# Small products of a hybrid attention and RWKV-7 layer, written with the whole 128 x 128 array

## The chip, the cores and the metric

The kernel runs on one core of a Trainium2 chip. The metric is device microseconds of one launch, the median of several runs; lower is better. A profile of one execution on the chip is read beside it. In it PE is the tensor engine's matmul, PEld its weight load, DVE the vector engine, ACT the scalar engine, POOL the GpSimd engine and SP the engine that issues most DMAs.

## The reference

One layer for 1024 tokens of width 1024. A combined projection feeds a sparse attention (eight heads) and an RWKV-7 recurrence (eight heads of 64); their outputs go through one output projection, and a feed-forward block of width 4096 follows. Cut to what the change touches:

```python
def dsa_attention(q, c_kv, q_idx, k_idx, w_idx, ...):
    inv_rms_k = lax.rsqrt(jnp.mean(k_full * k_full, axis=-1) + RMS_EPS)
    ...
    rel = jax.nn.relu(jnp.einsum('bthd,bsd->bths', qi, k_idx))      # index scores, 8 heads of 64
    score_idx = jnp.einsum('bth,bths->bts', wi, rel)
    score_idx = jnp.where(key_pos[None, :] < limit[:, None], score_idx, -jnp.inf)
    _, sel = lax.top_k(score_idx, 256)
    ...

def rwkv7_time_mix(p, ...):
    w_log = -jax.nn.softplus(-(w0 + jnp.tanh(xw) @ w2)) - 0.5
    decay = jnp.exp(-jnp.exp(w_log))
    a = jax.nn.sigmoid(a0 + xa @ a2)                                # xa: 64 columns
    kk = heads(k * k_k)
    kk = kk / jnp.maximum(jnp.sqrt(jnp.sum(kk * kk, axis=-1, keepdims=True)), 1e-12)
    def step(state, inp):
        sa = einsum('bhij,bhj->bhi', state, -kk_t)
        state = state * w_t + sa[..., None] * (kk_t * a_t) + v_t[..., None] * k_t
        return state, einsum('bhij,bhj->bhi', state, r_t)
    ...

def reference(x, c, ...):
    h = rms_norm(x, g_mix) * (1 + sc1) + sh1
    proj = h @ w_in
    x = x + gt1 * (concat([o_a, o_b]) @ w_out)
    h = rms_norm(x, g_ffn) * (1 + sc2) + sh2
    u = relu(h @ w_ff1)
    return x + gt2 * ((u * u) @ w_ff2)
```

## The kernel before

Tokens are worked on in two halves of 512. **The large products** (`dense`, `load_w`) keep weights stationary: a block of 128 x 128 weights is split into a high part `whi` (made by ACT) and a low part `wlo` (made by POOL or DVE), and the 512 tokens' activations, split likewise (`hh`, `hl`; in the feed-forward `uh`, `ul`), stream past. Each block gives three products of 128 rows, 128 columns and 512 streamed elements, here called dense products; there are 4608 of them and their PSUM tile is `ps_mm`. A product of plain float32 tiles stands in the trace as two hardware matmuls, one of the split tiles as one.

**The recurrence** (`rwkv_proj`, `rwkv_feat`, `rwkv_feat2`, `rwkv_inv`, `rwkv_chain`, `rwkv_out`) runs per half for four pairs of heads, each pair in eight chunks of 64 tokens. A chunk is a loop of dependences between PE and DVE: the products `Mt x Vbd` and `KR x H` fill `px`; DVE copies it to `Xb` (L659); the product with the inverse `TT` gives `pu` (L660), which DVE copies to `UV` (L661) and ACT to `Ub` (L663); the product of `BKn` and `UV` gives `ph`, with which DVE renews the state `H` (L669), on which the next chunk's `KR x H` waits. The product of `Lb` and `Ub` (L665, into rows 64 to 127 of `px`) gives the output, which ACT copies to `On`. `rwkv_inv` prepares the inverse `TT` of the next pair, mostly on DVE (`Y`, `ytmp`, L616 and L618).

**Sums of squares** per head (`stat`, L434) multiply by a matrix of 8 columns, one product for each pair of heads, 24 in all; `attn_proj` has two more with one column (the latent's sum, `pc`). **The second low-rank input** `xa` is multiplied by the 64 rows of `a2` (L516), once for each pair, 8 in all.

**The indexer** (`indexer`) scores 512 queries of each half against the keys, head by head. For each head and each block of 128 queries and up to 512 keys there are two products into `ps_f`: `qs x kiH`, where `qs` holds the queries' high parts in rows 0 to 63 and their low parts in rows 64 to 127 and `kiH` the keys' high parts twice, and `qs[0:64] x kiL`, of 64 rows. ACT takes the relu to `rl`, DVE adds it to the scores `sc` (L840). There are 80 such pairs of products, 16 in the first half and 64 in the second. After them comes a search for the 256th largest score, bit by bit, on DVE and ACT, then the attention.

What stands beside what on an engine is set by a scheduler of the framework when the kernel is built: every engine works off a fixed list in order. Between the small products of the recurrence and the indexer it puts dense products of the projections and of the first half's feed-forward. The second half's feed-forward stands last, with nothing else beside it.

Of the kernel before, what the change touches and what calls it, by code (L numbers as in the profile page):

```python
# [4 lines left out]
F32 = mybir.dt.float32  # L5
# [46 lines left out]
# column layout of the packed per-partition parameters  # L52
# [8 lines left out]
# column layout of the constants (they depend on shapes alone)  # L61
CC = {}
_n = 0
for _name, _w in (("ident", 128), ("oblk", 128), ("tri", 128), ("ind", 32), ("zmask", 128), ("yinit", 256),
                  ("dmat", 128), ("cdiag", 128)):
    CC[_name] = (_n, _w)
    _n += _w
NCC = _n
NCF = CC["zmask"][0]    # the columns before are needed as float32


def make_consts():
# [3 lines left out]
    def put(name, a):  # L76
        o, w = CC[name]
        c[:, o:o + w] = a
# [17 lines left out]
    ind = np.zeros((128, 4, 8))  # L96
    for j in range(4):
        ind[:64, j, 2 * j] = 1
        ind[64:, j, 2 * j + 1] = 1
    put("ind", ind.reshape(128, 32))  # L100
# [10 lines left out]
def body(tc, I, out, dbg=None):  # L111
# [21 lines left out]
    # ---------------------------------------------------------------- pools  # L133
# [11 lines left out]
    # ---------------------------------------------------------------- constants and parameters  # L145
# [25 lines left out]
    def power(t):  # L171
        """t**-0.5 in place"""
        G.tensor_tensor(t, t, mhalf.to_broadcast(list(t.shape)), ALU.pow)

    def newton(x, y, t):
        """y = x**-0.5 by Newton's steps from the halved bits"""
# [8 lines left out]
    def sigmoid(out, x, bias=0.0):  # L185
        """sigmoid(x + 2*bias) = (1 + tanh(x/2 + bias))/2"""
        A.activation(out, x, AF.Tanh, scale=0.5, bias=bias)
        EN(8).tensor_scalar(out, out, 1.0, 0.5, ALU.add, ALU.mult)
# [19 lines left out]
    a2w = cst.tile([128, 512], F32, name="a2w")  # L208
    nc.sync.dma_start(a2w[64:128], I["a2"])
# [5 lines left out]
    # persistent state  # L215
# [8 lines left out]
    # DRAM scratch  # L224
# [14 lines left out]
    # ---------------------------------------------------------------- modulation  # L239
# [6 lines left out]
    g1 = per.tile([128, 16], F32, name="g1")   # g*(1+sc) for the two norms  # L246

    def modulation4(j, q, pool, tag):
        """mod[:, 8j+4q ... 8j+4q+3], from 512 columns of w_ada"""
# [17 lines left out]
    def modulation_v(j, q, pool, tag):  # L267
        """the same, with the products away from the tensor engine"""
# [22 lines left out]
    # ---------------------------------------------------------------- x^T, norm, h^T  # L291
# [13 lines left out]
    def norm_first(hf, xp, xn, nb, tags):  # L305
        """x^T, each token over its rms, to the eight tiles of xn"""
# [37 lines left out]
    def norm_T(xT, n, n2, xp, hp):  # L344
        """the norm of x^T: sums over d by the tensor engine, four column groups at a time"""
# [16 lines left out]
        # over all partitions: out[d, t] = sum over t' of r1[t'] * (t' == t)  # L362
# [12 lines left out]
    # ---------------------------------------------------------------- dense product, weights stationary  # L375
    def load_w(w, row0, col0, M):
        """four row blocks of weights, as hi and lo"""
# [23 lines left out]
    # ---------------------------------------------------------------- RWKV-7  # L401
# [30 lines left out]
    def stat(ps, src, j):  # L432
        """sums over each head's rows of pair j, as rows 2j and 2j+1"""
        mmul(ps[0:8, :], C("ind", 8 * j, 8 * j + 8), src, start=(j == 0), stop=(j == 3))  # L434

    def inverse(ps, i, sl, scale, eps):
        """the -0.5th power of max(sum, eps) or of scale*sum + eps for eight rows of sums; to rnd[i]"""
# [17 lines left out]
    def rwkv_proj(hf, hT):  # L455
        """projections of group B, shifted; r, k, v to DRAM; the inverse norms of k*k_k"""
# [29 lines left out]
    def rwkv_feat(hf, j, L4, rp, bp):  # L486
        """features of head pair j; what the even pairs need lies in rp, so that they can run ahead"""
# [17 lines left out]
        # per-token decay exponents in natural layout  # L505
# [10 lines left out]
        mmul(pa, a2w[64:128, j * 128:j * 128 + 128], xa[64:128, :])  # L516
        # a = (1 + at)/2
# [30 lines left out]
        # kappa * W_{t-1}, with W_{-1} = 1 at a chunk's first token  # L548
# [50 lines left out]
    def rwkv_inv(hf, j, R, rp):  # L599
        mark('inv%d%d' % (hf, j))  # L600
        Lb, TT = R["Lb"], R["TT"]
# [46 lines left out]
    def rwkv_chain(hf, j, R, rp):  # L648
# [4 lines left out]
        for c in range(8):  # L653
# [6 lines left out]
            mmul(pu[0:64, 0:128], TT[:, c, :], flat(Xb))  # L660
            (A.copy if CE[1] == "a" else V.tensor_copy)(UV[0:64, c, :], pu[0:64, 0:128])  # L661
            for h in range(2):
                (V.tensor_copy if CE[2] == "v" else A.copy)(Ub[h * 64:h * 64 + 64, h, :], pu[0:64, h * 64:h * 64 + 64])  # L663
            mmul(ph[:, 0:128], BKn[:, c, :], UV[:, c, :])
            mmul(px[64:128, 0:128], Lb[:, c, 1, :], flat(Ub), start=False, stop=True, tile_position=(0, 64),  # L665
                 skip_group_check=True)
# [32 lines left out]
    # ---------------------------------------------------------------- sparse attention  # L699
    def attn_proj(hf, hT, rt):  # L700
        """projections of group A: q^, k^, v and the indexer's q and k to DRAM"""
# [26 lines left out]
        # latent, keys and values  # L728
# [6 lines left out]
        mmul(pc[0:1, :], ones128[:, 0:1], sq)  # L735
# [38 lines left out]
        # indexer keys and weights  # L774
# [14 lines left out]
    def indexer(hf, ap, mp):  # L789
        """additive masks (0 or -1e30) of the half's four query blocks"""  # L790
# [23 lines left out]
        kiL = ap.tile([64, SW], F32R, name="kiL", tag="kiL", bufs=1)  # L814
        A.copy(kiH[:, 0:SW], kir[:, 0:SW])
        V.tensor_tensor(kiL[:, 0:SW], kir[0:64, 0:SW], kiH[0:64, 0:SW].bitcast(F32), ALU.subtract)
# [3 lines left out]
        for h in range(8):  # L820
# [5 lines left out]
            for b in blocks:  # L826
                W = width(b)
                s_ = sc[b]
                for c0 in range(0, W, 512):
# [4 lines left out]
                    mmul(ps[:, 0:n], qs[0:64, tq], kiL[:, c0:c0 + n], start=False, stop=True)  # L834
# [9 lines left out]
        # the 256th largest score of each row, bit by bit in the order of the floats. The vector engine counts  # L844
        # (x >= c); the scalar engine sums sign(x - c), which is #(x > c) + #(x >= c) - W and so finds that score
# [439 lines left out]
```

## Time and profile before

| | |
|---|---|
| median of 3 runs | 1831.04 us (1826.63 to 1836.64) |
| span of the profiled execution | 1829.8 us |
| PE busy | 1661.3 us (91%), 8388 matmuls |
| PEld busy | 1200.9 us (66%) |
| DVE busy | 1160.2 us (63%) |
| ACT busy | 867.0 us (47%) |
| POOL busy | 467.8 us (26%) |
| granted TensorE clock, mean | 0.962 |

The profile gives the span from the first to the last instruction of its execution and no longer time for it; the median of the runs is 1.2 us above that span. The ends of matmuls are modelled, so a matmul's listed duration runs into the next one; the time that a product takes of the engine is read from the starts of successive products. An operation named `ps_f<-kiL,iqs 64*128 64x512` is a product into the tile `ps_f` that uses 64 rows and 128 columns of the array (`64*128`) and streams 512 elements.

### The profile page before, as it was taken

What the parts mean: (1) busy time and instruction counts of PE and PEld (TensorE: products, weight loads), DVE (VectorE), ACT (ScalarE), POOL (GpSimd) and SP (SyncE); (2) the same over time, 40 slices, a digit from 0 to 9 for tenths busy, and PEclk for the clock granted to TensorE, in tenths of its full rate; (3) what the DMA queues carried; (4) which work ended last, traced back from release to release, by engine and by line L of the source; (5) the groups of instructions that cost most, each with busy time, mean ns of one, the idle gap of its engine ahead of it and who ended that gap; (6) DMA issues with size and microseconds to landing.
All of it is one profiled execution on the core that took longest, in us unless ns stands there. A gap on an engine that the chain in (4) does not pass through costs nothing. (4 is left out here: it accounts for less than half of the span.)

```text
span 1829.8 us, 25015 instructions
## 1 busy us (share of the span) xinstructions
PE 1661.3 (91%) x8388; PEld 1200.9 (66%) x8388; DVE 1160.2 (63%) x2981; ACT 867.0 (47%) x1760; POOL 467.8 (26%) x390
## 2 busy tenths in 40 slices
PE   5997889898978988989997789799999999999998
PEld 2674546556653656656555668577786788888887
DVE  4777789845898868986579956877212343333333
ACT  4323353443556655335664687576425252525251
POOL 2445322323241142333312344110344300000000
PEclk9997999998989999999998899899999999999999
DMA  9795344224334643111311223341532343333332
GB/s 311 255 286 181 87 140 144 74 70 133 98 94 149 193 142 106 45 47 47 87 35 52 65 80 110 93 110 47 167 98 74 88 138 93 98 93 98 97 94 75
DMA packets 279366, 205.53 MB, mean 112 GB/s; under 512 B 33811, under 2 KB 234643, under 8 KB 279238
## 3 DMA queue, kind: packets, MB, share of 16 engines
q1 hardware_dynamic: 268482, 184.68, 34.1%
q10 hardware_dynamic: 10628, 19.24, 2.9%
q8 instruction: 66, 1.08, 0.2%
q14 instruction: 62, 0.51, 0.1%
q0 software_dynamic: 128, 0.01, 0.0%
HBM read 175.11 MB, written 28.78 MB: 111 GB/s over the span
## 5 line engine op out<-in xcount | busy, mean ns | idle before, releaser
L384 POOL TENSOR_TENSOR wlo<-wraw,whi 128x512 fp32r<-128x512 f32 x256 | 338.5, 1326 | 737.6 <-ACT whi L382 625.9
L120 PE MATMUL ps_mm<-hh,whi 128*128 128x512 f32 (+1 forms) x1024 | 423.2, 414 | 21.7 <-ACT ur L1061 6.9
L382 ACT CAST whi<-wraw 128x512 fp32r<-128x512 f32 x384 | 235.5, 616 | 400.6 <-PE ps_mm L120 383.7
L120 PE MATMUL ps_mm<-hl,whi 128*128 128x512 f32 (+1 forms) x1024 | 421.7, 412 | 3.6 <-DVE hl L328 1.9
L120 PE MATMUL ps_mm<-hh,wlo 128*128 128x512 f32 (+1 forms) x1024 | 421.0, 411 | 0.7 <-POOL wlo L384 0.6
L120 PEld LDWEIGHTS ps_mm<-hh,whi 128*128 128x128 f32 (+1 forms) x1024 | 197.7, 194 | 79.8 <-issue 20.2
L120 PEld LDWEIGHTS ps_mm<-hl,whi 128*128 128x128 f32 (+1 forms) x1024 | 197.7, 193 | 54.9 <-issue 13.9
L120 PEld LDWEIGHTS ps_mm<-hh,wlo 128*128 128x128 f32 (+1 forms) x1024 | 198.1, 193 | 50.9 <-issue 12.3
L120 PE MATMUL ps_mm<-uh,whi 128*128 128x512 f32 x512 | 207.3, 406 | 15.3 <-DVE acc L895 10.0
L120 PE MATMUL ps_mm<-ul,whi 128*128 128x512 f32 x512 | 206.8, 404 | 2.0 <-DVE ul L1077 2.0
L120 PE MATMUL ps_mm<-uh,wlo 128*128 128x512 f32 x512 | 206.1, 403 | 0.7 <-POOL wlo L384 0.6
L384 DVE TENSOR_TENSOR wlo<-wraw,whi 128x512 fp32r<-128x512 f32 x128 | 88.2, 689 | 130.8 <-ACT whi L382 130.8
L874 ACT ACTIVATE jka<-sc,canda 128x1024 bf16<-128x1024 f32 (+1 forms) x93 | 90.2, 970 | 87.9 <-DVE canda L872 68.2
L120 PEld LDWEIGHTS ps_mm<-uh,whi 128*128 128x128 f32 x512 | 98.0, 192 | 40.5 <-ACT jka L874 10.8
L1083 DVE SCALAR_TENSOR_TENSOR xT<-ps_mm,mod,xT 128x512 f32<-128x512 f32 x64 | 47.9, 749 | 108.5 <-PE ps_mm L120 108.4
L120 PEld LDWEIGHTS ps_mm<-ul,whi 128*128 128x128 f32 x512 | 98.1, 192 | 25.5 <-DVE ul L1077 2.8
L120 PEld LDWEIGHTS ps_mm<-uh,wlo 128*128 128x128 f32 x512 | 98.2, 192 | 24.9 <-issue 1.8
L1077 DVE TENSOR_TENSOR ul<-ur,uh 128x512 fp32r<-128x512 f32 x64 | 47.9, 748 | 71.8 <-ACT uh L1076 71.7
L618 DVE TENSOR_TENSOR Y<-Y,ytmp 128x60 f32<-128x60 f32 (+24 forms) x248 | 75.7, 305 | 6.2
L616 DVE TENSOR_TENSOR ytmp<-Lu,Y 128x60 f32<-128x60 f32 (+24 forms) x248 | 72.6, 293 | 6.1
L982 DVE CUSTOM_DVE_ANT_0 L<-ps_f,mk 128x512 f32<-128x512 f32 (+3 forms) x96 | 52.0, 552 | 26.2 <-PE ps_c L1000 15.6
L988 ACT ACTIVATE L<-L,m 128x128 f32<-128x128 f32 (+7 forms) x64 | 49.7, 777 | 30.9 <-DVE m L985 21.0
(319 smaller groups left out, 2563.6 us busy)
## 6 DMA issues: line engine op xcount, KB each, us to landing
wraw<-in_w_ff_dram SPq DMA_DIRECT2D x256, 256.0 KB, 2.8
wraw<-in_w_in_dram SPq DMA_DIRECT2D x92, 256.0 KB, 3.4
mraw<-in_w_ada_dram SPq DMA_DIRECT2D x64, 256.0 KB, 5.0
mraw<-in_w_ada_dram SPq DMA_DIRECT2D x16, 512.0 KB, 10.7
wraw<-in_w_out_dram SPq DMA_DIRECT2D x32, 256.0 KB, 2.9
rkvd<-shy ACTq DMA_DIRECT2D x24, 256.0 KB
xin<-in_x_dram SPq DMA_DIRECT2D x8, 512.0 KB, 5.5
v<-rkvd SPq DMA_DIRECT2D x16, 256.0 KB
```

The lines of the kernel that those rows point to most:

```text
L120: r = T.matmul(out, lhsT, rhs, start=start, stop=stop, **kw)
L382: (A.copy if HE[GRP[0]] == "a" else V.tensor_copy)(hi[:, :, 0:M], raw[:, :, 0:M])
L384: (V if LE[GRP[0]] == "v" or LE[GRP[0]] == "m" and GRP[1] else G).tensor_tensor(lo[:, :, 0:M], raw[:, :, 0:M], hi[:, :, 0:M].bitcast(F32), ...
L616: V.tensor_tensor(tv, Lu[:, c, 0:c].unsqueeze(2).to_broadcast([128, c, n]), Y[:, c, t0:8].unsqueeze(1).to_broadcast([128, c, n]), ALU.mult)
L618: V.tensor_tensor(Y[:, 0:c, t0:8], Y[:, 0:c, t0:8], tv, ALU.subtract)
L874: A.activation(jka[:, 0:width(b)], sc[b], AF.Sign, scale=-1.0, bias=0.0 if bit == 31 else canda.bitcast(F32)[:, i:i + 1], accum_out=ca[:, ...
L982: V.tensor_tensor_reduce(L[:, c0:c0 + n], ps[:, 0:n], masks[b][:, c0:c0 + n], 1.0, -3e38, ALU.add, ALU.max, m2[:, pc:pc + 1])
L988: A.activation(L[:, 0:W], L[:, 0:W], AF.Exp, bias=m2[:, 2:3], accum_out=m2[:, 3:4])
L1077: V.tensor_tensor(b, r, a.bitcast(F32), ALU.subtract)
L1083: V.scalar_tensor_tensor(xT[:, d, :], ps, mod[:, 40 + d:41 + d], xT[:, d, :], ALU.mult, ALU.add)
```

## The change

Six kinds of product that used 64 rows, or 64, 8 or 1 columns of the array, are written with 128 rows and 128 columns. What is added is zero rows, or columns whose results nobody reads:

- `stat`: the 8-column matrix becomes a slice of 128 columns out of 134, zero but for two columns, so that the rows 2j and 2j+1 of the sums stay where they were; all 128 rows of the PSUM tile are written and 8 read.
- `a2`: `a2w` gets 64 zero rows by a memset, and `xa` is loaded with all 128 rows (256 KB for 128 KB, twice).
- the product with `TT`: the weights are the 64 columns of chunk c and the 64 of chunk c+1 (`TT` has a ninth, zero block), and 64 of 128 result rows are read.
- the product with `Lb`: the weights are both 64-column halves of `Lb`; the results of the unread half are added to rows 0 to 63 of `px`, which have been copied by then.
- `pc`: 128 columns of ones for one.
- the indexer's second product: `kiL` is made for 128 rows instead of 64, and multiplies all of `qs`. (Here the added rows are not zero: they add the product of the two low parts.)

The rest of the diff takes out comments and docstrings, which moves a line number by one from L120 on.

```diff
-                  ("tri", 128), ("ind", 32), ("zmask", 128), ...
+                  ("tri", 128), ("ind", 134), ("zmask", 128), ...
...
-    ind = np.zeros((128, 4, 8))
-    for j in range(4):
-        ind[:64, j, 2 * j] = 1
-        ind[64:, j, 2 * j + 1] = 1
-    put("ind", ind.reshape(128, 32))
+    ind = np.zeros((128, 134))
+    ind[:64, 6] = 1
+    ind[64:, 7] = 1
+    put("ind", ind)
...
+    G.memset(a2w[0:64], 0.0)
     nc.sync.dma_start(a2w[64:128], I["a2"])
...
-        mmul(ps[0:8, :], C("ind", 8 * j, 8 * j + 8), src, start=(j == 0), stop=(j == 3))
+        mmul(ps, C("ind", 6 - 2 * j, 134 - 2 * j), src, start=(j == 0), stop=(j == 3))
...
-        mmul(pa, a2w[64:128, j * 128:j * 128 + 128], xa[64:128, :])
+        mmul(pa, a2w[:, j * 128:j * 128 + 128], xa)
...
-            mmul(pu[0:64, 0:128], TT[:, c, :], flat(Xb))
+            mmul(pu[:, 0:128], flat(TT[:, c:c + 2, :]), flat(Xb))
...
-            mmul(px[64:128, 0:128], Lb[:, c, 1, :], flat(Ub), start=False, stop=True, tile_position=(0, 64),
-                 skip_group_check=True)
+            mmul(px[:, 0:128], flat(Lb[:, c, :, :]), flat(Ub), start=False, stop=True, skip_group_check=True)
...
-        mmul(pc[0:1, :], ones128[:, 0:1], sq)
+        mmul(pc, ones128, sq)
...
-        kiL = ap.tile([64, SW], F32R, name="kiL", tag="kiL", bufs=1)
+        kiL = ap.tile([128, SW], F32R, name="kiL", tag="kiL", bufs=1)
         A.copy(kiH[:, 0:SW], kir[:, 0:SW])
-        V.tensor_tensor(kiL[:, 0:SW], kir[0:64, 0:SW], kiH[0:64, 0:SW].bitcast(F32), ALU.subtract)
+        V.tensor_tensor(kiL[:, 0:SW], kir[:, 0:SW], kiH[:, 0:SW].bitcast(F32), ALU.subtract)
...
-                    mmul(ps[:, 0:n], qs[0:64, tq], kiL[:, c0:c0 + n], start=False, stop=True)
+                    mmul(ps[:, 0:n], qs[:, tq], kiL[:, c0:c0 + n], start=False, stop=True)
...
-        nc.sync.dma_start(xa[64:128], xwd[64:128, sl])
+        nc.sync.dma_start(xa, xwd[:, sl])
...
-        TT = [TT0, bp.tile([128, 8, 64], F32, name="TT1")]
+        TT = [TT0, bp.tile([128, 9, 64], F32, name="TT1")]
...
-    TT0 = rp.tile([128, 8, 64], F32, name="TT0")
+    TT0 = rp.tile([128, 9, 64], F32, name="TT0")
```

The scheduler writes other lists for the changed products. On PE, in the fifth chunk of the second pair of heads of the second half, this stands before from the product of `UV` to the next product of `H` (a row gives the result's rows and columns):

```order
L120 MATMUL ps_c<-UV,BKn 128x128
L120 MATMUL ps_o<-Ub_5738,Lb 64x128
L120 MATMUL ps_mm<-hh,whi 128x512
L120 MATMUL ps_mm<-hl,whi 128x512
L120 MATMUL ps_mm<-hh,wlo 128x512
L120 MATMUL ps_o<-Vbd,Mt 128x128
L120 MATMUL ps_mm<-hh,whi 128x512
L120 MATMUL ps_mm<-hl,whi 128x512
L120 MATMUL ps_o<-H_119,KR 128x128
```

And this stands there in the changed kernel:

```order
L119 MATMUL ps_c<-UV,BKn 128x128
L119 MATMUL ps_o<-Ub_5739,Lb 128x128
L119 MATMUL ps_mm<-hh,whi 128x512
L119 MATMUL ps_mm<-hl,whi 128x512
L119 MATMUL ps_o<-Vbd,Mt 128x128
L119 MATMUL ps_mm<-hh,wlo 128x512
L119 MATMUL ps_mm<-hh,whi 128x512
L119 MATMUL ps_o<-H_120,KR 128x128
```

One dense product fewer stands between the two. Over all chunks 65 dense products leave the recurrence for later places: ahead of the second half's first product with `kiL` stand 1508 dense products before and 1443 now, and the two lists are level again at the 2832nd, in the middle of the feed-forward blocks. In the second half's index scores, PE's list before reads, at the 49th to 52nd product with `kiL`:

```order
L120 MATMUL ps_f<-kiH,iqs 128x512
L120 MATMUL ps_f<-kiL,iqs 128x512
L120 MATMUL ps_mm<-uh,whi 128x512
L120 MATMUL ps_f<-kiH,iqs 128x128
L120 MATMUL ps_f<-kiL,iqs 128x128
L120 MATMUL ps_mm<-ul,whi 128x512
L120 MATMUL ps_mm<-uh,wlo 128x512
L120 MATMUL ps_f<-kiH,iqs 128x512
L120 MATMUL ps_f<-kiL,iqs 128x512
L120 MATMUL ps_f<-kiH,iqs 128x256
L120 MATMUL ps_f<-kiL,iqs 128x256
```

And now:

```order
L119 MATMUL ps_f<-kiH,iqs 128x512
L119 MATMUL ps_f<-kiL,iqs 128x512
L119 MATMUL ps_mm<-hl,whi 128x512
L119 MATMUL ps_mm<-hh,wlo 128x512
L119 MATMUL ps_f<-kiH,iqs 128x128
L119 MATMUL ps_f<-kiL,iqs 128x128
L119 MATMUL ps_f<-kiH,iqs 128x512
L119 MATMUL ps_f<-kiL,iqs 128x512
L119 MATMUL ps_f<-kiH,iqs 128x256
L119 MATMUL ps_f<-kiL,iqs 128x256
```

The pairs of products come in the same order, with other dense products beside them; in the whole stretch from the first to the last product with `kiL` of this half there are 71 dense products in both lists.

## Rows read from the trace of the kernel before

**Rows 1.** Page, busy time of each engine, share of the span, instructions.
```profile
PE 1661.3 (91%) x8388; PEld 1200.9 (66%) x8388; DVE 1160.2 (63%) x2981; ACT 867.0 (47%) x1760; POOL 467.8 (26%) x390
```
**Rows 2.** Stretches: busy us of each engine (instructions), granted clock, DMA share, GB/s.
```profile
core 0: us, PE busy (x) PEld busy (x) DVE busy (x) ACT busy (x) POOL busy (x), PEclk, DMA share, GB/s
210.00:360.00 150.00, 132.29 (x824) 83.11 (x823) 132.60 (x422) 68.32 (x182) 44.78 (x38) 0.99 0.39 118
380.00:420.00 40.00, 39.80 (x199) 25.39 (x198) 16.62 (x54) 17.84 (x46) 8.97 (x7) 0.98 0.20 54
665.00:865.00 200.00, 180.85 (x1146) 120.67 (x1144) 166.20 (x467) 92.06 (x227) 60.34 (x49) 0.97 0.22 64
889.50:954.50 65.00, 65.00 (x199) 34.09 (x198) 47.27 (x75) 41.53 (x81) 9.50 (x7) 1.00 0.14 41
954.50:1050.00 95.50, 74.37 (x277) 57.57 (x278) 92.19 (x267) 50.56 (x92) 30.12 (x22) 0.88 0.20 58
447.50:473.50 26.00, 25.98 (x76) 15.31 (x77) 18.85 (x26) 14.92 (x29) 6.45 (x5) 0.87 0.31 92
```
**Rows 3.** Chain that ended last: start us, us, what.
```profile
1475.04 334.24 PE ps_mm L120 x1457
```
**Rows 4.** Timeline, PE, second half's index scores: start us, us, product.
```profile
920.21 0.39 PE L120 MATMUL ps_f<-kiH,iqs 128*128 128x512 f32 x1
920.52 0.50 PE L120 MATMUL ps_f<-kiL,iqs 64*128 64x512 f32 x1
920.95 0.49 PE L120 MATMUL ps_f<-kiH,iqs 128*128 128x512 f32 x1
921.38 0.50 PE L120 MATMUL ps_f<-kiL,iqs 64*128 64x512 f32 x1
921.80 0.50 PE L120 MATMUL ps_mm<-ul,whi 128*128 128x512 f32 x1
922.14 0.39 PE L120 MATMUL ps_mm<-uh,wlo 128*128 128x512 f32 x1
```
**Rows 5.** Timeline, PEld, two microseconds on: start us, us, weight load, idle before.
```profile
922.14 0.19 PEld L120 LDWEIGHTS ps_f<-kiH,iqs 128*128 128x128 f32 x1
922.68 0.18 PEld L120 LDWEIGHTS ps_f<-kiL,iqs 64*128 64x128 f32 x1 [0.35 <-issue]
```
**Rows 6.** Tile kiL: product, count, ns min/median/max, first and last start, forms.
```profile
L120 PE MATMUL ps_f<-kiL,iqs x80: 324/492/792, 447.9 to 954.3; 64*128 64x512 f32 x48, 64*128 64x384 f32 x16, 64*128 64x128 f32 x8, 64*128 64x256 f32 x8
```
**Rows 7.** Timeline, PE, a chunk of the second half's third pair of heads.
```profile
788.62 0.38 PE L120 MATMUL ps_o<-H,KR 128*128 128x128 f32 x2
788.76 0.48 PE L120 MATMUL ps_mm<-hh,whi 128*128 128x512 f32 x1
789.07 0.40 PE L120 MATMUL ps_mm<-hl,whi 128*128 128x512 f32 x1
...
789.53 0.40 PE L120 MATMUL ps_mm<-hh,whi 128*128 128x512 f32 x1
789.77 0.40 PE L120 MATMUL ps_mm<-hl,whi 128*128 128x512 f32 x1
790.10 0.43 PE L120 MATMUL ps_c<-Xb,TT 128*64 128x128 f32 x2
790.46 0.50 PE L120 MATMUL ps_mm<-hh,wlo 128*128 128x512 f32 x1
790.80 0.40 PE L120 MATMUL ps_mm<-hh,whi 128*128 128x512 f32 x1
```
**Rows 8.** Waits of PE: us in total, times, longest us.
```profile
PE ps_c L120 <- DVE Xb L659: 11.3, 14, 3.1
PE ps_c L120 <- DVE UV L661: 4.2, 8, 1.2
```
**Rows 9.** Weight loads by shape: line, operation, shapes, count | busy us, mean ns | idle before.
```profile
L120 PEld LDWEIGHTS ps_o<-Ub,Lb 128*64 128x64 f32 x128 | 12.5, 138 | 13.6 <-ACT Ub L663 6.3 <-issue 2.6 <-ACT whi L382 0.9
L120 PEld LDWEIGHTS ps_c<-Xb,TT 128*64 128x64 f32 x128 | 12.2, 135 | 37.3 <-DVE Xb L659 26.1 <-issue 6.1 <-ACT BKn L597 1.7
L120 PEld LDWEIGHTS ps_dx<-asq,con 128*8 128x8 f32 x32 | 1.5, 87 | 12.7 <-ACT asq L712 10.8 <-ACT kr L764 0.8 <-issue 0.6
```

More of the change, by code (lines that the diff above doesn't have):

```diff
@@ L63 @@
 _n = 0
-for _name, _w in (("ident", 128), ("oblk", 128), ("tri", 128), ("ind", 32), ("zmask", 128), ("yinit", 256),
+for _name, _w in (("ident", 128), ("oblk", 128), ("tri", 128), ("ind", 134), ("zmask", 128), ("yinit", 256),
                   ("dmat", 128), ("cdiag", 128)):
@@ L600, in rwkv_inv @@
         mark('inv%d%d' % (hf, j))
-        Lb, TT = R["Lb"], R["TT"]
+        Lb, TT = R["Lb"], R["TT"][:, 0:8, :]
         Ld = rp.tile([128, 8, 32], F32, name="Ld", tag="Ld", bufs=1)
```

## The prediction

> **What bounds the kernel now.** I read the page's busy times first, then busy time by stretches, the chain that ended last, PE's timeline in two places, and the waits. PE is busy 91% of the span, no other engine over 63% [rows 1]. From 1475 us on the chain holds almost nothing but dense products: 1457 of them in 334.24 us, 0.229 us each [rows 3]. That is the pace of a PE that never waits, and time saved ahead of this tail shortens the span in full. The reader should look for what lies above that pace earlier.
>
> In the second half's index scores (889.5 to 954.5 us) PE is the bound: busy 65.0 of 65.0 us, against 47.3 for DVE and 41.5 for ACT [rows 2]. In the recurrence PE and DVE are close: 132.3 and 132.6 of 150 us, 180.9 and 166.2 of 200; only in the last pair of the first half (380 to 420) has DVE room, with 16.6 of 40 [rows 2]. The search after the scores belongs to DVE, with 92.2 of 95.5 us [rows 2].
>
> **What a small product costs today.** Take the starts in the scores: 920.21, 920.52, 920.95, 921.38, 921.80, 922.14 [rows 4]. Five products take 1.93 us; at 0.229 they would take 1.15. The extra 0.78 us belongs to four changes between 128 rows and 64, so 0.196 us each. The parts can be seen: from `kiH` to `kiL` 0.31 (0.08 over the pace: the array empties first), from `kiL` to the next 0.42 or 0.43 (its own weights are loaded in sight, and the array empties again), and after the change back 0.34 (a full-size product that also had to wait for its weights). On PEld the load for `kiL` begins only at 922.68, after 0.35 us of idleness put down to no releaser [rows 5]; loads between equal shapes begin one product ahead.
>
> In the recurrence `H,KR`, which has the full shape, and the dense product behind it take 0.45 us together (788.62 to 789.07); `Xb,TT` with 64 columns and the one behind it take 0.70 (790.10 to 790.80), and ahead of it 0.33 passes instead of 0.24 [rows 7]. So such a product costs 0.34 us more than a full one, if PE isn't waiting for data anyway.
>
> **The change part by part**, on PE's time first:
> - `kiL`: 64 products in the second half's scores, 16 in the first (80 in all [rows 6]), two changes of shape each. 128 x 0.196 = 25.1 us and 32 x 0.196 = 6.3 us. The 128 rows stream no longer than 64, since only the streamed elements count.
> - `Xb,TT` and `Ub,Lb`: 64 products each (128 hardware matmuls in each row [rows 9]). 128 x 0.34 = 43.5 us at most. Where PE stands waiting, nothing is gained in front, and the wider load costs 0.19 [rows 5] less 0.135 to 0.138 [rows 9], some 0.055 us more. PE waits so for `Xb` 14 times, 11.3 us, and for `UV` 8 times, 4.2 us [rows 8].
> - 24 sums and the 2 of the latent: 0.39 for two changes less 0.10 for a load of 128 columns instead of 8 (0.19 against 0.087 [rows 5, 9]), some 0.3 each, 7.8 us.
> - `a2`: 8 x 0.39 = 3.1 us. Its memset, the doubled load of `xa` (twice 128 KB more) and 102 more columns of constants are ready long before use, and DVE's `kiL` is two instructions on more partitions at the same length; I cost them at nothing, at most 1 us together.
>
> Together 85.8 us of PE time. What of it reaches the end:
> - Second half's scores: PE needs 65.0 - 25.1 = 39.9, less than DVE's 47.3 [rows 2]. DVE ends last now: between 47.3 and 65, and I take 50, since PE has two `ps_f` banks and DVE will not be fed without gaps. -15.
> - First half's scores: 26.0 - 6.3 = 19.7, against DVE's 18.9 [rows 2]: -5.
> - Recurrence: DVE has 17.4 and 33.8 us idle in the two long stretches [rows 2]. Its idle time is where it waits for PE in the loop; half of it, 25.6, is a guess between nothing and all. In the pair at 380 us, where DVE has room, 8 x 2 x 0.34 = 5.4. Together -31.
> - 65 dense products leave the recurrence for the feed-forward, where PE has nothing to hide them: 65 x 0.229 = +14.9. Part of the 31 is thus only moved.
> - Sums, latent and `a2`: half of 10.9, as the sums also wait for ACT's squares (10.8 us of idle loads [rows 9]): -5.5.
>
> Sum: -15 - 5 - 31 + 14.9 - 5.5 = -41.6. The profiled execution's span of 1829.8 becomes 1788.2. The median lies 1.2 above the span, so I forecast **1789 us**.
>
> What is late next: in the scores DVE's accumulation (L840). In the recurrence the wait for `Xb`, behind which PE's list holds `Xb,TT` and two or three dense products, and behind these `UV,BKn`, for which `H` and thus the next chunk waits. The search starts earlier and is no shorter.
>
> The Trainium skill, "TensorEngine Tiling (Array Packing)", section "Key Properties", says that tiles of the array work independently, so that a weight load and a matmul in different tiles run side by side. It speaks against this change: by it a 64-row product would run beside its neighbour, and filling the array would give that up. The starts in the scores don't bear it out, as `kiL` holds its successor back by 0.43 us and not by less than 0.229.
>
> **Rivals.**
> 1. The recurrence gives nothing net: the loop of copies and waits sets its time, and what it loses is only the moved dense products. For it: DVE at 88% in the first stretch and the 22 waits [rows 2, 8]. Against: the 0.33 us ahead of `Xb,TT` with its successor ready [rows 7]. Then -15 - 5 - 5.5: 1806.
> 2. PE's list decides almost everywhere, and all but the scores' DVE limit comes back: 15 + 6.3 + 43.5 + 10.9 = 75.7: 1755. For it: the waits for `Xb` and `UV` are only 15.5 us [rows 8]. Against: DVE would have no idle time left.
> 3. Slower: PE now waits more in the recurrence and its clock is granted less often. The search shows it: PE busy 74 of 95.5 us, granted clock 0.88, against 0.97 to 0.99 in the recurrence [rows 2]. PE's 353 busy us there (132 + 40 + 181) would become 353 x (0.98/0.88 - 1) = 40 us longer; with the moved 14.9 us and 128 x 0.055 = 7 us of wider loads, against 25.5 saved elsewhere, +36: 1867. From a clock of about 0.94 downwards (353 x (0.98/0.94 - 1) = 15, and 15 + 22 - 25.5 = +11) it decides the sign. Against it: the same columns stream in less time, which leaves PE no idler than now.
> 4. The change doesn't do what it says: small products cost nothing by their shape and run beside their neighbours. Then 80 full products are added, 80 x 0.229 = 18, and the loads 7: 1856. Only the 0.34 us after each `kiL` [rows 4], which belongs to a full-shape product, speaks strongly against it, and it is enough. It is what the page cited above would lead to.
>
> **Chances.** Forecast 0.60 (its own range 1774 to 1798), rival 1 0.20, rival 2 0.09, rival 3 0.06, rival 4 0.05. A difference of 0.5%, 9 us, is about what a measurement of this kernel can tell from none. Faster by more holds the forecast, rival 2 and most of rival 1, whose 25 us allow for a reshuffled list that costs 16: 0.87. Within 0.5%: 0.06, from rival 1's slow end and 3 and 4 half-way. Slower: 0.07. The range of 1760 to 1817 leaves out most of rival 2 and the slower cases.
>
> **What would show it.** In the profile after: `kiH`, `kiL` and dense products starting 0.23 us apart where nothing waits, and the loads for `kiL` one product ahead; the scores' stretch at 48 to 53 us with DVE nearly full; behind `Xb,TT` 0.45 us instead of 0.70; more of PE's waits put down to `Xb` and `UV`; a longer stretch of pure dense products at the end, by some 15 us. The forecast is wrong if the starts after `kiL` keep the 0.34, if the scores stay at 65 us, if the recurrence's eight pairs take as long as now, or if the granted clock there falls below 0.94.

## The result, and the profile after

The changed kernel takes 1808.04 us (median of 4 runs, 1806.42 to 1810.30) against 1829.9 us for the kernel before (4 runs, 1826.63 to 1836.64): a ratio of 0.9878, with an interval of 0.9859 to 0.9898. That is 22 us faster; the forecast was 42. The profiled execution's span went from 1829.8 to 1804.6 us, and its granted clock from 0.962 to 0.966.

The page's busy times answer to [rows 1]: PE loses 47.5 us, PEld and DVE stay within 6 us, ACT loses 7.5 us and POOL gains 12.5.

```profile
PE 1613.8 (89%) x8388; PEld 1206.4 (67%) x8388; DVE 1159.7 (64%) x2981; ACT 859.5 (48%) x1760; POOL 480.3 (27%) x391
```

The same stretches as in [rows 2], found by the same products (recurrence of the first half, its last pair, recurrence of the second half, second half's scores, the search's first 98 us, first half's scores), in the same columns:

```profile
210.80:352.60 141.80, 121.64 (x801) 83.52 (x800) 127.77 (x413) 65.22 (x177) 43.51 (x36) 0.99 0.41 123
373.30:402.50 29.20, 28.82 (x147) 20.50 (x146) 13.20 (x44) 13.79 (x39) 6.40 (x5) 1.00 0.27 72
651.80:835.60 183.80, 158.35 (x1069) 108.73 (x1068) 155.31 (x451) 80.60 (x206) 53.89 (x45) 0.99 0.22 64
863.30:911.70 48.40, 47.09 (x199) 31.95 (x198) 46.45 (x73) 39.21 (x84) 9.31 (x7) 1.00 0.17 50
911.70:1010.00 98.30, 75.52 (x286) 58.36 (x285) 95.25 (x274) 50.57 (x91) 31.13 (x22) 0.88 0.20 59
431.60:451.30 19.70, 18.73 (x80) 13.93 (x80) 18.73 (x26) 14.45 (x28) 6.74 (x5) 1.00 0.44 129
```

The second half's scores went from 65.0 to 48.4 us, with DVE busy for 46.5 of them; the first half's from 25.0 to 19.7, with DVE busy for 18.7. That DVE sets the pace there is read from the waits too. Before, PEld stood idle 72 times with no releaser; now it stands for ACT's relus, and ACT stands for DVE, which still has to read an older `rl` (us in total, times, longest us; the first line is before, the others after):

```profile
PEld ps_f L120 <- issue: 20.5, 72, 0.4
PEld ps_f L119 <- ACT rl L835: 12.8, 35, 0.9
ACT rl L835 <- DVE sc L839: 3.7, 7, 0.9
```

PE's 47.1 busy us there don't speak against it, as a matmul's listed duration runs into the next one.

The recurrence's stretches are shorter too, by 14 and 12 us from first to last product (205.3 to 191.8 and 196.1 to 183.7), but hold fewer dense products, and PE now has 20 and 25 us in the long stretches in which it isn't busy, against 18 and 19 before.

PE's timeline in the scores, beside [rows 4]: each product starts 0.23 us after the one before, where it waits for nothing.

```profile
892.71 0.39 PE L119 MATMUL ps_f<-kiL,iqs 128*128 128x512 f32 x1
892.94 0.40 PE L119 MATMUL ps_mm<-hl,whi 128*128 128x512 f32 x1
893.17 0.39 PE L119 MATMUL ps_mm<-hh,wlo 128*128 128x512 f32 x1
893.40 0.40 PE L119 MATMUL ps_f<-kiH,iqs 128*128 128x512 f32 x1
893.63 0.40 PE L119 MATMUL ps_f<-kiL,iqs 128*128 128x512 f32 x1
```

And PEld there, beside [rows 5]: the load for the product of 893.63 begins at 893.40, one product ahead.

```profile
893.18 0.19 PEld L119 LDWEIGHTS ps_f<-kiH,iqs 128*128 128x128 f32 x1
893.40 0.19 PEld L119 LDWEIGHTS ps_f<-kiL,iqs 128*128 128x128 f32 x1
```

In the recurrence the product with `TT` and the dense one behind it now take 0.45 us (769.38 to 769.83), where [rows 7] had 0.70:

```profile
769.16 0.39 PE L119 MATMUL ps_mm<-hl,whi 128*128 128x512 f32 x1
769.38 0.38 PE L119 MATMUL ps_c<-Xb,TT 128*128 128x128 f32 x2
769.52 0.48 PE L119 MATMUL ps_mm<-hh,wlo 128*128 128x512 f32 x1
769.83 0.39 PE L119 MATMUL ps_mm<-hh,whi 128*128 128x512 f32 x1
```

PE's waits, beside [rows 8]: those for `UV` trebled, those for `Xb` are more often and a little less in total.

```profile
PE ps_c L119 <- DVE UV L661: 13.1, 17, 2.6
PE ps_c L119 <- DVE Xb L659: 9.9, 21, 0.9
```

The chain that ended last still holds the same run of dense products as [rows 3], 24.1 us earlier and no longer:

```profile
1450.98 333.27 PE ps_mm L119 x1457
```

Where the 25 us of span arose is seen from when the same product starts in both traces (us, and after less before). These are single executions, and unchanged stretches differ by some us from one to the next: the first recurrence's first product starts at 207.2 to 213.5 us in the traces of the kernels before, after and of the first five experiments.

| | before | after | |
|---|---|---|---|
| first half's recurrence, last product | 417.0 | 402.5 | -14.5 |
| first half's scores, last product | 472.9 | 451.2 | -21.7 |
| first half's attention, last product with `kh` | 644.1 | 631.4 | -12.7 |
| second half's recurrence, last product | 863.2 | 835.6 | -27.6 |
| second half's scores, last product | 954.3 | 911.6 | -42.7 |
| second half's attention, last product with `kh` | 1275.7 | 1239.4 | -36.3 |
| 2437th dense product (lists level again) | 1304.6 | 1280.9 | -23.7 |
| 2833rd dense product | 1395.9 | 1372.1 | -23.8 |
| end | 1829.8 | 1804.6 | -25.2 |

Between the first half's scores and the end of its attention 9 us are given back; 8 of the moved dense products are done there, some 1.8 us, and the rest isn't traced further. Between the second half's scores and the end of its attention 6.4 us are given back, with as many dense products there as before (789 for 791); the cause isn't traced. Behind that another 12.6 us are given back: at the attention's last product with `kh` 67 dense products fewer have been done than before (2303 for 2370), and by the 2437th they are made up for. From there on the two lists of PE agree in names and shapes, earlier than at the 2832nd named above.

### The profile page after: what moved, and what is told of

It is laid out like the page before. It is cut to its first block, busy times and chain, and to the rows that moved or that the text cites. A ratio compares the mean times of both kernels' runs of the same rounds, so it can differ in the third digit from the quotient of the medians.

```text
span 1804.6 us, 25007 instructions
## 1 busy us (share of the span) xinstructions
PE 1613.8 (89%) x8388; PEld 1206.4 (67%) x8388; DVE 1159.7 (64%) x2981; ACT 859.5 (48%) x1760; POOL 480.3 (27%) x391
## 5 line engine op out<-in xcount | busy, mean ns | idle before, releaser
L384 POOL TENSOR_TENSOR wlo<-wraw,whi 128x512 fp32r<-128x512 f32 x256 | 350.9, 1375 | 699.4 <-ACT whi L382 583.7
L119 PE MATMUL ps_mm<-hh,whi 128*128 128x512 f32 (+1 forms) x1024 | 421.9, 413 | 25.6 <-ACT whi L382 6.0
L119 PEld LDWEIGHTS ps_mm<-ul,whi 128*128 128x128 f32 x512 | 98.0, 191 | 29.2 <-DVE ul L1076 7.3
L1076 DVE TENSOR_TENSOR ul<-ur,uh 128x512 fp32r<-128x512 f32 x64 | 44.0, 690 | 74.6 <-ACT uh L1075 74.4
L663 ACT COPY Ub<-ps_c 64x64 f32<-64x64 f32 x128 | 26.2, 205 | 83.7 <-DVE UV L661 76.3
```

The costliest lines, as they stand in the source:

```text
L119: r = T.matmul(out, lhsT, rhs, start=start, stop=stop, **kw)
L384: (V if LE[GRP[0]] == "v" or LE[GRP[0]] == "m" and GRP[1] else G).tensor_tensor(lo[:, :, 0:M], raw[:, :, 0:M], hi[:, :, 0:M].bitcast(F32), ...
L1076: V.tensor_tensor(b, r, a.bitcast(F32), ALU.subtract)
```

## The experiments

The theory after the result: the scores gave what was forecast; in the recurrence PE's saved time became waiting; the recurrence shortened only by the dense products that moved out, and these are paid for later. The rival: the recurrence did give its 16 us net, and something else ate them.

**The scores' edit alone**, on the kernel before:

```diff
-        kiL = ap.tile([64, SW], F32R, name="kiL", tag="kiL", bufs=1)
+        kiL = ap.tile([128, SW], F32R, name="kiL", tag="kiL", bufs=1)
...
-                    mmul(ps[:, 0:n], qs[0:64, tq], kiL[:, c0:c0 + n], start=False, stop=True)
+                    mmul(ps[:, 0:n], qs[:, tq], kiL[:, c0:c0 + n], start=False, stop=True)
```

> The kernel before with the change to the indexer's second product alone (kiL with 128 rows). PE's list keeps its dense products where they were. Theory (a change of the array's shape costs 0.2 us, and DVE ends the second half's scores): the stretch of the 64 products shrinks from 65 to 48-50 us, that of the 16 from 25 to 20, and since nothing is moved the end comes 18 to 22 us earlier, ratio 0.988 to 0.990. Rival (the gain of the scores is lost again in the search behind them): the stretches shrink alike, but the end comes less than 10 us earlier, ratio over 0.994.

Measured: 1806.0 us, ratio 0.9865 (0.9844 to 0.9886). This one edit is worth 24 us, as much as the whole change. Its stretches, first and second half's recurrence and second half's scores:

```profile
213.00:361.00 148.00, 131.58 (x818) 82.31 (x817) 130.32 (x418) 67.61 (x180) 45.23 (x38) 0.99 0.40 120
662.70:859.50 196.80, 177.48 (x1115) 117.87 (x1114) 163.65 (x461) 89.20 (x222) 60.53 (x48) 0.97 0.21 63
885.00:935.00 50.00, 47.58 (x200) 31.96 (x199) 47.71 (x75) 38.82 (x83) 10.71 (x7) 1.00 0.18 53
```

**`Lb`'s edit alone** (the full-width product with `Lb` on the kernel before, nothing else):

> The kernel before with the product of Lb and Ub alone written with 128 columns. This edit alone makes the scheduler move the 65 dense products out of the recurrence. Theory (the moved products are paid for again in the feed-forward, 14.9 us): the recurrence's eight pairs get 12 to 22 us shorter, the stretch from the second half's attention to its norm some 13 us longer, and the end comes between 7 us earlier and 3 us later, ratio 0.996 to 1.002. Rival (moved products are hidden in waits of PE that are there anyway): the end comes 12 to 22 us earlier, ratio 0.988 to 0.993.

Measured: 1827.16 us, ratio 0.9982 (0.9967 to 0.9996): inside the theory's range, and the rival's 0.988 to 0.993 is out. Its profiled execution took 1838.2 us, so only the lengths of stretches are read from it. The recurrences are 3.6 and 9.1 us shorter, 12.7 together. From the second half's last product with `kh` to the 2833rd dense product it takes 133.1 us, 12.9 us more than before, as the theory has it. This length is the clearest sign of the moved products: 120.0 to 120.5 us in the five traces with the list of before (before, and the experiments with the scores alone, all but `Lb`, the sums alone and all but the loop's edits), 133.1 here and 132.6 in the whole change.

This is the edit that makes the scheduler move 65 dense products; that it does so because the product now writes all 128 rows of `px`, of which the copy to `Xb` reads rows 0 to 63, is likely but not tested. In the four others just named PE's list is that of before, product by product but for the shapes.

**All but `Lb`'s edit**:

> The whole change but for the product of Lb and Ub, which stays at 64 columns; the dense products stay where they were in the kernel before. Theory (moved products are paid for again): the recurrence gains some 8 to 13 us from Xb,TT, nothing is given back, and the end comes 26 to 36 us before that of the kernel before, ratio 0.980 to 0.986, so this version beats the whole change. Rival (the place of the dense products doesn't matter): it loses what Ub,Lb brought, and the end comes 8 to 14 us earlier, ratio 0.992 to 0.996.

Measured: 1806.04 us, ratio 0.9864 (0.9845 to 0.9882): between the two ranges written down, and as fast as the scores' edit alone. As PE's list is the one of before, the recurrence can be compared product by product:

```profile
208.00:357.50 149.50, 128.76 (x819) 85.41 (x818) 131.81 (x419) 68.81 (x182) 44.88 (x39) 0.99 0.39 118
658.70:855.50 196.80, 175.59 (x1117) 121.28 (x1116) 162.62 (x462) 89.24 (x222) 60.89 (x48) 0.96 0.21 63
882.50:932.00 49.50, 47.40 (x199) 31.77 (x198) 47.33 (x74) 37.88 (x81) 10.88 (x7) 1.00 0.18 54
```

The stretches take 149.5 and 196.8 us, against 148.0 and 196.8 without the edit of `TT`. DVE's busy time is the same to 1.5 us. Where PE's saved time is found is shown by the account below.

**Sums, `a2` and the latent's sum alone**:

> The kernel before with the sums of squares, the latent's sum and the product with a2 alone written with 128 rows and columns. Theory as forecast: half of their 10.9 us of PE time comes back, the end 3 to 7 us earlier, ratio 0.996 to 0.998. Rival (they stand where PE waits for ACT or DVE anyway): within 2 us, ratio 0.999 to 1.001.

Measured: 1827.5 us, ratio 0.9981 (0.9965 to 0.9996), some 3 us. It lies between the two ranges, and the interval reaches into both.

**All but the two edits in the loop** (`TT` and `Lb`):

> The change without its two edits in the recurrence's loop (the products with TT and Lb keep their 64 columns); kiL, the sums, a2 and the latent's sum are padded. Theory (in the loop the saved PE time turns into waits, elsewhere it reaches the end): the gains of the two parts measured alone, 24 and 3 us, add: 1803 to 1804 us, ratio 0.983 to 0.987, as fast as the whole change or 2 to 5 us faster; recurrence stretches as long as with the scores' edit alone, 148 and 197 us. Rival (the loop's edits are worth what the forecast gave them, 16 us net, and something else ate it): 16 us slower than the whole change, 1820, ratio 0.995.

Measured: 1805.96 us, ratio 0.9862 (0.9840 to 0.9884). So the rival's 1820 is out: the loop's two edits bring nothing at the end (what the recurrence gained on the way is told in the next section). The 3 us of the sums can't be seen on top of the 24. The versions with the scores' edit are all alike within their intervals (0.9862 to 0.9878), so none beats the changed kernel by what can be measured.

An account of PE's time over the whole span shows why they are alike. From the starts, shapes and streamed elements of all 8388 products, each gap between two is put down to a change of shape, with a price of up to 0.20 us (near the 0.199 measured by itself below; less where fewer columns are loaded), and otherwise to waiting. The number of changes and the sum are read from the trace; how the sum divides between the two columns rests on that price.

| kernel | changes of shape | their cost, us | waits, us | sum |
|---|---|---|---|---|
| before | 698 | 122.4 | 263.9 | 386.3 |
| scores alone | 538 | 90.3 | 272.1 | 362.4 |
| all but the loop's edits | 486 | 82.5 | 278.7 | 361.2 |
| all but `Lb` | 361 | 60.9 | 300.5 | 361.4 |
| the whole change | 238 | 39.5 | 321.0 | 360.5 |

The streams, 1425.5 us in each, are not in the sum. The scores' edit saves 32.1 us and 8.2 of them become waits; of the other 50.8 us that the whole change saves, 48.9 become waits.

**Half of DVE's adds left out** in the second half's scores, with the scores' edit:

```diff
-                    else:
+                    elif not hf or h < 4:
                         V.scalar_tensor_tensor(s_[:, c0:c0 + n], rl[:, 0:n], wn[hf][:, b, h:h + 1],
```

> The kernel before with kiL padded, leaving out DVE's accumulation of heads 4 to 7 in the second half's index scores. Theory (with kiL padded DVE's accumulation ends last there): DVE's busy time in the stretch falls from 47 to about 25 us, and the stretch from 48 to 50 us to 40 to 43, where PE's products and ACT's relus (39 us) end it. Rival (PE ends last still, by its own products): 48 to 50 us as before.

Measured: 1804.32 us (one run, span 1802.5). The stretch as such can't be read as expected: the scheduler started the search among the scores and put more dense products there, so its last product came at 950.3. But scores and search together end earlier: the second half's attention starts at 1120.4, against 1135.8 with all the adds. So DVE bounds scores and search taken together; for the scores' stretch alone, as the theory has it, this run doesn't decide, and its being set by DVE rests on the busy times and waits above. Of these 15.4 us, 3.0 reach the end, less than single runs tell apart: the dense products that had stood beside the search are done later.

**A quarter of these adds on POOL**, as a multiply and an add of their own:

```diff
+                    if gp_ and h:
+                        G.tensor_scalar(rl[:, 0:n], rl[:, 0:n], wn[hf][:, b, h:h + 1], 1.0, ALU.mult, ALU.mult)
+                        G.tensor_tensor(s_[:, c0:c0 + n], rl[:, 0:n], s_[:, c0:c0 + n], ALU.add)
```

> The change without the loop's two edits, with a quarter of the second half's accumulation (one block of 128 queries, heads 1 to 7) on POOL as a multiply and an add. Theory (DVE ends last in the scores): DVE does about 37 us there, the stretch goes from 49 to 41 to 44 us, and the kernel is 5 to 8 us faster than its neighbour in this call, 1796 to 1799 us, ratio 0.981 to 0.983. Rival (POOL's two instructions for each head are slow, and ACT's relu waits for its tile): the stretch stays at 49 us or grows, ratio 0.985 to 0.990.

Measured: 1813.36 us, ratio 0.9896 (0.9874 to 0.9917), 7 us slower than the version without POOL's part: the rival's side. The stretch took 55.1 us. DVE did 57 instructions there instead of 75 and was no less busy (48.2 us), because each became longer. Groups by line: engine, operation, shapes, count, busy us, mean ns. DVE with its adds alone:

```profile
L840 DVE SCALAR_TENSOR_TENSOR sc<-rl,wn,sc 128x512 f32<-128x512 f32 x33 | 26.4, 821 | 0.5 <-ACT rl L836 0.2
L840 DVE SCALAR_TENSOR_TENSOR sc<-rl,wn,sc 128x384 f32<-128x384 f32 x7 | 4.3, 609 | 0.0
```

and beside POOL's:

```profile
L844 DVE SCALAR_TENSOR_TENSOR sc<-rl,wn,sc 128x512 f32<-128x512 f32 x25 | 25.6, 1044 | 4.1 <-ACT rl L837 3.9
L844 DVE SCALAR_TENSOR_TENSOR sc<-rl,wn,sc 128x384 f32<-128x384 f32 x6 | 6.8, 1127 | 0.0
```

The same add of 384 elements takes 1127 ns instead of 609 in the mean. Inside this one trace the means come apart: of the six adds of 384 elements, the three with no instruction of POOL beside them took 0.60 to 0.61 us, and the three with one 1.61 to 1.70. The 25 adds of 512 elements show the same, 0.74 us for the seven without and 1.16 for the others in the mean. So it is POOL's work beside them that makes them long. The rival had given another reason, ACT's relu waiting for POOL; what ACT's `rl` waits for here is DVE (6.9 us). This agrees with the Trainium skill, "SBUF — State Buffer", section "SBUF: two separate sides", by which DVE's instructions with two inputs from SBUF and those of GpSimd that read SBUF lock each other out of a shared port.

**Half of the inverse's steps left out**, on the version without `Lb`'s edit:

```diff
-        for c in range(31, 0, -1):
+        for c in range(31, 15, -1):
```

> The change without Lb's edit, leaving out half of the steps by which DVE prepares the inverse for the next pair of heads. Theory A (DVE's sum of work, loop copies and inverse, sets the recurrence's time): the first three pairs of each half get shorter by about 15% (a chunk from 4.9 to 4.2 us), the last pair of each half, which has no inverse beside it, does not. Theory B (the loop's own latency through PE, with the dense products queued in it, sets it): the chunks keep 4.8 to 5.0 us, DVE's idle time grows instead, and the recurrence's stretches stay at 149 and 197 us to within the dense products that the list moves.

Measured: 1795.4 us (one run). The recurrences, the first one in two parts:

```profile
193.00:332.00 139.00, 127.04 (x813) 84.71 (x812) 113.47 (x346) 66.04 (x178) 44.02 (x38) 0.98 0.43 127
340.00:375.00 35.00, 33.04 (x159) 22.38 (x159) 19.44 (x53) 18.41 (x47) 15.74 (x12) 1.00 0.24 68
625.00:805.00 180.00, 163.32 (x1056) 116.95 (x1054) 127.20 (x341) 75.58 (x199) 55.83 (x45) 0.92 0.26 81
```

DVE lost 18 and 35 us of work there. A chunk, from one new state to the next, still took 4.65 us in the mean, against 4.75: theory A's 4.2 is out. That leaves theory B's latency of the loop through PE as the better account of a chunk, but its stretches of 149 and 197 us became 139 and 181. What got shorter are above all the gaps between pairs, which theory B hadn't foreseen: before the first half's last pair 9.0 us instead of 24.8, before the second half's second pair 11.7 instead of 23.7. There the loop waits for the inverse: in the version without `Lb`'s edit the first of these gaps begins at 355 us, DVE works on the inverse until 372 us, and the list has filled the wait with 38 dense products, where 9 stand now. Of the second half's recurrence, which ended 50 us earlier, 10 us reached the end; 126 dense products fewer stand ahead of the scores behind it (1382 for 1508) and are done later.

**The price of a change of shape by itself**: 24 unread products in each of seven groups, A to G, behind the changed kernel's last one (168 in all, not 144 in six groups).

> The changed kernel with 144 products that nobody reads behind the last one, 24 in each of six groups: A full products (128 rows, 128 columns, 512 streamed); B full and 64 rows in turn; C 64 rows only; D 64 rows in turn from the upper and the lower half, into two banks; E full and 64 columns in turn; then F a full one and a plain float32 one of 128 columns and 128 streamed in turn, and G the same with 64 columns. Theory (the change of shape costs, not the small product; 0.196 us for each change of rows): A 0.21 to 0.23 us for each product, B 0.41 to 0.43, C 0.21 to 0.23 like A, D 0.21 to 0.23, E 0.37 to 0.43; G longer than F by 0.30 to 0.36 for each turn. Rival (a small product costs by itself, or its neighbour's weights come late): C as dear as B. Rival by the rule of independent tiles: D 0.11 to 0.13, two products side by side.

Measured, us from start to start: A 0.227; B 0.428 and 0.425; C 0.227; D 0.113; E 0.230; a turn of F 0.459, of G 0.788. So a 64-row product between 64-row products costs what a full one does, and each change of rows costs 0.199 us; the forecast had 0.196. G is 0.33 us longer than F, for which it had 0.34. Two expectations failed. The rival by independent tiles had D right: there the products run two at a time; the timeline, `ps_f` from the upper rows and `ps_c` from the lower:

```profile
1825.17 0.39 PE L119 MATMUL ps_f<-uh,ul 64*128 64x512 f32 x1
1825.30 0.39 PE L119 MATMUL ps_c<-uh,ul 64*128 64x512 f32 x1
1825.39 0.39 PE L119 MATMUL ps_f<-uh,ul 64*128 64x512 f32 x1
1825.54 0.39 PE L119 MATMUL ps_c<-uh,ul 64*128 64x512 f32 x1
1825.62 0.39 PE L119 MATMUL ps_f<-uh,ul 64*128 64x512 f32 x1
```

And in E, where the 64 columns are of the split type that the dense products use, the narrow product costs nothing extra; in G, of plain float32, it does. E and G differ in the streamed elements too (512 and 128), which no run separates from the type. A turn of G takes 0.79 us, 1839.70 to 1840.49, with a change on either side:

```profile
1839.70 0.43 PE L119 MATMUL ps_f<-uf 128*64 128x128 f32 x2
1840.06 0.49 PE L119 MATMUL ps_f<-uh,ul 128*128 128x512 f32 x1
1840.49 0.43 PE L119 MATMUL ps_f<-uf 128*64 128x128 f32 x2
```

**One of three dense products left out**, on the version without `Lb`'s edit:

```diff
-                mmul(ps[0:M], hi[:, k, 0:M], rl(K), start=False, stop=False)
```

> The change without Lb's edit, leaving out one of every three dense products (weights' high part with the activations' low part), 3072 instead of 4608. Theory (a chunk's 4.75 us are 2.9 us of the loop's own steps and 1.8 us of queueing behind dense products on PE and behind other work on DVE, and DVE's half was shown not to set it): a chunk takes 4.1 to 4.5 us, most of the gain in the step from the new state to the next product with it, which falls from 0.58 to 0.2 to 0.4 us. Rival (DVE's queue, or the copies, set the loop): a chunk keeps 4.6 to 4.8 us. The whole kernel becomes some 1536 x 0.229 = 350 us shorter at most, which is no finding.

Measured: 1710.58 us (one run). The theory's 4.1 to 4.5 us for a chunk is out: it takes 4.95. But this doesn't confirm the rival, for two things changed at once. The scheduler put other dense products in the loop (5.8 for each chunk instead of 7.6), and the granted clock fell. Both recurrences and the search:

```profile
221.00:370.00 149.00, 124.22 (x738) 84.80 (x737) 123.25 (x404) 63.43 (x172) 41.09 (x35) 0.84 0.38 113
680.00:865.00 185.00, 155.44 (x960) 107.61 (x959) 152.16 (x421) 82.80 (x198) 67.41 (x54) 0.88 0.22 61
978.00:1203.00 225.00, 154.75 (x530) 112.90 (x528) 176.43 (x441) 134.68 (x248) 97.56 (x69) 0.83 0.29 85
```

With 328 us of streams gone (1425.5 to 1097.8 in the account above), the waits rose by 233 us (300.5 to 533.6), and the span fell by 95. What sets the loop's time between PE's queue and DVE's is left open.

## Why the prediction was right, and where it was too large

The time lies 19 us above the forecast, inside the range, and within 2 us of rival 1's 1806. That the range held was in part luck: it was wide enough for rival 1, which had a chance of 0.20, and the step on which forecast and rival 1 differ went the rival's way. By its steps:

- **The cost of a change of shape** was right: 0.196 us read, 0.199 measured by itself; 85.8 us of PE time in all forecast, 82.9 by the account (122.4 to 39.5), which uses that price, so that it confirms the number of changes. The price doesn't hold for every narrow product (E).
- **The scores** were right in size, and the cause fits the waits. Forecast -15 for the second half, with DVE ending last at 50 us; the edit alone gave 50.0 us. First half -5, measured 25.0 to 19.6. The whole edit gave 24 us instead of 20.
- **The recurrence's -31 is the step that failed.** "Half of it, 25.6, is a guess between nothing and all": at the end it was nothing, as the version without the loop's edits is as fast (1805.96 for 1808.04). The last pair with room gave 1.4 (31.4 to 30.1 us from first to last product) with `TT` alone, for which half of the 5.4 was forecast, and 2.2 with `Lb` too (29.2), where it also holds 6 dense products fewer. The 0.34 us that a narrow product cost was PE's time, not the loop's. The loop's own steps show it, in means over the 56 chunks that follow another, us:

| step | before | all but `Lb` | after |
|---|---|---|---|
| new `H` to the load for `H,KR` | 0.593 | 0.581 | 0.598 |
| that load to the copy to `Xb` | 0.840 | 0.851 | 0.839 |
| copy's end to the load for `Xb,TT` | 0.152 | 0.115 | 0.061 |
| that load to the copy to `UV` | 0.876 | 0.936 | 0.940 |
| copy's end to the load for `UV,BKn` | 0.178 | 0.110 | 0.129 |
| that load to the renewal of `H` | 0.849 | 0.855 | 0.719 |
| DVE's three operations | 1.302 | 1.302 | 1.300 |
| sum | 4.79 | 4.75 | 4.59 |

Of the 0.34 us the loop gets 0.037 ahead of `Xb,TT` and 0.068 behind it, and gives back 0.060 for the wider load, which now stands in sight behind the copy: the 0.055 us that the prediction priced for "where PE waits", but counted nowhere in the sum. In all 56 x 0.04 = 2 us, and even that isn't clear of the spread: in six traces whose loop has none of the two edits a chunk takes 4.76 to 4.79 us.

In the whole change a chunk takes another 0.16 us less, or 0.09 in the second trace of the same loop (4.66 us, the run with the test products), and holds one dense product fewer (6.5 for 7.6). The count alone doesn't explain it: the second half's last pair has 36 for 77 and takes 32.9 us for 33.7, its third pair has 69 for 58 and takes 36.0 for 41.2. From first to last product the two recurrences are 26 us shorter than before, 20 in the second trace, of which the moved products are 15. What is left, 5 to 11 us, doesn't reach the end either: between the second half's last score and its last product with `kh` the two traces need 327.8 and 327.9 us, against 318.1 to 321.4 in the five with the list of before. So here the rival of the experiments is right in part: something eats a gain of the recurrence, and what it is stays open.
- **The 65 moved products** were right: 14.9 us forecast, 12.6 seen to be given back behind the second half's attention, and 12.9 with `Lb`'s edit alone. But they are paid for ahead of the 2437th product, not in the tail of pure dense products, which is as long as before; there the prediction's own sign to look for was wrong. Leaving out `Lb`'s edit ends the second half's recurrence 19.3 us later and the whole 1.1 us earlier.
- **The sums**: -5.5 forecast, some 3 us alone, not to be seen beside the scores. The memset and the larger loads, costed at nothing, are in this run too.
- **The rivals**: rival 1 is what happened at the end; its reason, a loop of copies and waits, is what the table shows for `TT`. Rival 3 is out, as the clock didn't fall (0.962 and 0.966 in the two traces), but in the run with fewer dense products it did. By its own numbers the sign would have turned at a clock of about 0.97 already, not 0.94: 353 x (0.98/0.97 - 1) + 22 - 25.5 is about 0. Rival 4 is out for products between full ones (B). The rule behind it, from the Trainium skill, "TensorEngine Tiling (Array Packing)", section "Key Properties", is not: small products side by side do overlap (D), and the same section says that a change of tiling mode empties the engine, which B's 0.199 us agrees with.

So the sum would have been -20, -5.5 and nothing net for the recurrence. The mistake was to let a share of PE's saved time reach the end in a stretch where PE, with 132 of 150 us busy, already waited for a loop.

## What to carry to other kernels

Saved time on an engine counts only in stretches where that engine ends last: ask of each edit which wait it shortens on the loop, not how much work it takes away. Here a product of 64 rows between full ones paid for two changes of shape, so try to fill such a product up where the engine is the bound. Where the engine waited it brought nothing at the end, and the wider load then stood in the loop (0.060 us a chunk). When work moves out of a stretch as filler, look for the place where it is done instead before counting the stretch as shorter.

## What the runs showed of the hardware

- 64-row products of the split type from the two halves of the rows, into two banks, start 0.113 us apart, two in the time of a full one; alternated with full ones they cost 0.43 us each.
- Narrow weights of 64 columns cost nothing extra in a product of the split type (0.230 us) and 0.33 us a turn in plain float32, with loads of the same 134 ns; the first streamed 512 elements and the second 128.
- DVE's add of 384 elements took 0.60 to 0.61 us with POOL idle and 1.61 to 1.70 us beside an instruction of POOL; POOL's own add of 512 took 1555 ns.
- With a third of the dense products gone, the granted clock in the first recurrence went from 0.99 to 0.84, and a chunk took longer (4.95 for 4.75 us), with other dense products beside it.
